# The keys' decay sums of a forgetting attention: by a thin product on TensorE for each head, or by a broadcast through memory

## The chip, the cores and the metric

One core of a Trainium2 chip. The metric is the device time of the whole program in microseconds, as the median of several executions.

## The reference

One call runs 256 tokens of width 1024, in float32, through two blocks. The first is a feed-forward layer, a mixer (chunked attention and pooling), and a second feed-forward layer. The second block is a forgetting attention ("fox") and a sparse latent attention ("dsa"), each followed by a layer norm. What is computed in the forgetting attention, with 8 heads of width 128:

```python
q, k, v, f_logit, gate = split(x @ w_in)
log_f = log_sigmoid(f_logit + b_f)                # [token, head]
cum = cumsum(log_f, axis=token)
s = (q @ k.T) * 128 ** -0.5 + cum[query, head] - cum[key, head]
s = where(key <= query, s, -inf)
o = softmax(s) @ v
y = (silu(gate) * o) @ w_out
```

So a score has three terms beside the product of query and key: a sum that belongs to the query (one number for each row of a tile of scores), a sum that belongs to the key (one number for each column, the same in all rows), and the causal mask. The change is about the second.

## The kernel before

The 256 tokens are two tiles of 128. A weight matrix is cut into units of two 128-row blocks of up to 512 columns (512 KB). SP's queue loads the units in the order of use into four buffers; ScalarE makes of each a rounded part (`whi`, line 195) and VectorE the rest (`wlo`, line 196), into eight buffers each. A product with the weights is three products on TensorE (line 162): low part of x by high part of w, high by low, high by high. Both tiles use a unit before it is given up, and the splits run up to eight units ahead of the use.

The order of the work on TensorE is written with a clock of the kernel's own: each product adds its estimated time to it, and the attention's pieces are put in a heap with a due time (the table DUE) after what they follow. After each half of a unit the pieces that are due are emitted between the products with weights. The framework's planner then fixes, before the program runs, the order of each engine's instructions and all waits and buffers; on the chip each engine works through its list in order.

The forgetting attention runs in this order: the blocks of k, q, and [f | v]; after the first block of [f | v] the logits of the gates are turned into `log_f`; `cums` (line 728) makes the running sums, and two more blocks of v pass; then the two gate blocks of the first tile, with the first tile's attention between their products, and the two of the second tile with the second's (`attend`, line 809). Scores are made in groups, of 4 heads and 128 keys for the first tile (two groups), and of 2 heads and 256 keys for the second (four groups). A group has one of the two PSUM banks that have the name `sc`; these banks serve the products with v too.

`cums` makes by small products the sums both ways: `cq`, a token to a partition, for the queries, and a copy of [8 heads, 256 keys] for the keys. Of the latter a rounded part goes to rows 0 to 7 of a tile `cum` (ScalarE), and the rest, by VectorE and GpSimd, to rows 32 to 39. `E` is a constant of 40 rows that holds -1 at a head's two rows. In `scores` (line 758) the product of E's column, broadcast to 128 columns, with `cum` puts the key's sum, negated, into all rows of the bank, and the head's own product is added to it. VectorE adds the query's sum and the mask on the way out of PSUM:

```python
self.mm(ps[:, i, :], E[:, h:h + 1].to_broadcast([40, P]), cum[:, 0:nk], True, False, 1)
if t == 0:
    self.mm(ps[:, i, :], qT[:, h, :], kT[:, h, :], False, True)
else:
    self.mm3(ps[:, i, :], qTs, kTs, False, True, (slice(None), h), (slice(None), h))
nc.vector.scalar_tensor_tensor(s[:, i, :], ps[:, i, :], cq[t][:, h:h + 1],
                               self.cmask[:, S - nk:S], op0=ALU.add, op1=ALU.add)
```

For the first tile a head's own product is one in full float32 (two records in the trace), for the second it is three of the split parts. Then come the maximum over keys (VectorE, line 419), the exponentials (ScalarE, line 421), transposes on TensorE (line 177), the product with v, and the gating.

Of the kernel before, what the change touches and what calls it, by code (L numbers as in the profile page):

```python
# [16 lines left out]
P = 128  # L17
# [18 lines left out]
# column blocks of the products with x on the left, in the order in which they are used  # L36
FFN_CH = [(512 * j, min(512, DFF - 512 * j)) for j in range((DFF + 511) // 512)]
MIX_CH = [(1536, 512), (512, 512), (0, 512), (1024, 512)]           # u k q v
FOX_CH = [(1024, 512), (1536, 512), (0, 512), (512, 512),           # k0 k1 q0 q1
          (0, 344), (344, 344), (688, 344),                          # of [f | v]  # L40
          (3080, 512), (3592, 512)]                                  # gate
DSA_CH = [(0, 372), (372, 372),                                      # of [ki | qi | wi | kr | ckv]
          (0, 512), (512, 512), (1768, 512), (2280, 512)]            # q gate


def unit_list():
    """(matrix, first k-tile, k-tiles, first column, columns) in the order of use."""
    u = []

    def block(m, c0, w, k0=0, k1=KT, n=None):  # L50
        n = n or (UK * (512 // w) if 512 % w == 0 else UK)
        for k in range(k0, k1, n):
            u.append((m, k, min(n, k1 - k), c0, w))

    def ffn(i):
        for c0, w in FFN_CH:
            block(f"gate{i}", c0, w, n=1 if i == 1 and c0 == 0 else None)
            block(f"up{i}", c0, w)
        for n in range(2):
            block(f"down{i}", 512 * n, 512, 0, FT)  # L60

    ffn(1)
    for c0, w in MIX_CH:
        block("mix", c0, w)
    for k0 in (4, 0):
        for n in range(2):
            block("mix_out", 512 * n, 512, k0, k0 + 4)
    ffn(2)
    for i, (c0, w) in enumerate(FOX_CH):
        block("fox_fv" if 4 <= i < 7 else "fox", c0, w)  # L70
    for n in range(2):
        block("fox_out", 512 * n, 512)
    for i, (c0, w) in enumerate(DSA_CH):
        block("dsa_idx" if i < 2 else "dsa", c0, w)
    for n in range(2):
        block("dsa_out", 512 * n, 512)
    return u
# [6 lines left out]
# When, in us of the tensor engine's work after what it follows, a piece of work takes its turn.  # L84
# [29 lines left out]
class Kern:  # L114
    def __init__(self, ctx, tc, A):
        self.tc, self.nc, self.A, self.ctx = tc, tc.nc, A, ctx
        pool = lambda name, **k: ctx.enter_context(tc.tile_pool(name=name, bufs=1, **k))
        self.cp = pool("const")
        self.wp = pool("w")
        self.xp = pool("x")  # L120
        self.ps = pool("ps", space=bass.MemoryType.PSUM)
        self.now = 0.0
        self.heap, self.fired, self.blocked = [], set(), {}
        self.seq = 0
        self.n_dma = self.n_split = self.used = 0
        self.raw, self.W = {}, {}
        off = 0
        self.off = []
        for (_, _, nk, _, w) in UNITS:
            self.off.append(off)  # L130
            off += P * nk * w

# [5 lines left out]
    def when(self, keys, us, fn):  # L138
        """fn, us after all of the keys are fired."""
        keys = [k for k in keys if k not in self.fired]  # L140
        if not keys:
            self.later(us, fn)
        else:
            self.blocked.setdefault(keys[0], []).append((keys[1:], us, fn))
# [23 lines left out]
    def mm3(self, out, a, b, start, stop, ai=slice(None), bi=slice(None)):  # L168
        """a.T @ b from the parts (hi, lo) of a and b, taken at ai and bi."""
        (ah, al), (bh, bl) = a, b  # L170
        self.mm(out, al[ai], bh[bi], start, False, 1)
        self.mm(out, ah[ai], bl[bi], False, False, 1)
        self.mm(out, ah[ai], bh[bi], False, stop, 1)
# [39 lines left out]
    def half(self, acc, lhs, i, first, last, kbase=0, cols=None):  # L213
        """acc += lhs.T @ unit i, for one tile of tokens; lhs: (hi, lo) of [P, k-tile, P]."""
# [18 lines left out]
    def split_psum(self, hi, lo, src, scale=None):  # L233
        """hi + lo = src (a PSUM tile), times a column for each of its blocks if scale is given."""
# [15 lines left out]
    def split_scaled(self, dst, src, f):  # L250
        """hi + lo = src f, f a column or a number."""
        hi, lo = dst
        self.nc.scalar.activation(hi, src, AF.Copy, scale=f)
        self.nc.vector.scalar_tensor_tensor(lo, src, f, hi.bitcast(F32), op0=ALU.mult, op1=ALU.subtract)
# [5 lines left out]
    def open_xT(self, t):  # L260
        """After the last product with x[t]: what follows is written to x's operand."""
# [3 lines left out]
    def put_T(self, dst, t, src, k0, n, scale=None):  # L265
        """dst k-tiles k0.. of tile t = transposed blocks of src ([P, n * P])."""
# [19 lines left out]
    def rstd(self, t, src=None, n=D, eps=EPS):  # L286
        """1 / rms of each token of x[t]."""
# [12 lines left out]
    def first_chunk(self, u0, n, pool, gain):  # L300
        """The first block: x's transposes come from memory, a pair of k-tiles at a time."""
# [26 lines left out]
    def chunk(self, u0, n, first_gain=None):  # L328
        """The product of x with one block of columns (units u0 .. u0+n), tile by tile.

        Yields t when tile t is complete. With first_gain the second half of x's transposes
        is made in between, where the vector engines have it ready."""
# [82 lines left out]
    def softmax_part(self, pool, s, nh, nk, l, col):  # L415
        """exp(s - max) for nh heads ([P, nh, nk]) in place; row sums into l[:, col..]."""
# [7 lines left out]
    def p_T(self, pool, s, nh, nk, split=False):  # L424
        """Transposes of s: [k, head, k-tile, q], or the parts of [k, k-tile, head, q]."""
# [20 lines left out]
    def mixer(self, u, gain, next_gain):  # L446
        self.stage = "mix"
        nc, tc, A = self.nc, self.tc, self.A
        with tc.tile_pool(name="mix", bufs=1, reuse_waits="tile") as pool:
# [11 lines left out]
            # of the first tile's products whole operands, of the second's the parts  # L461
# [34 lines left out]
            def scores(t, b):  # L496
                """Heads of one half of t: both halves of the array's rows at once, to two banks."""
# [104 lines left out]
    def layer_norm(self, t, o, g, b, out=None):  # L602
        """x[t] = LN(alpha x[t] + o); o: PSUM banks of 512 columns, or of 512, 256, 256."""
# [29 lines left out]
    def silu_gate(self, pool, acc, out, hr):  # L633
        """out = y (1 + tanh(z / 2)) = 2 silu(z) / (z / y); hr: half of z / y, or None for a half."""
# [5 lines left out]
    def out_proj(self, u, after, last=False):  # L640
        """o = og @ w_out, a tile at a time; after(t, (half, half))."""
# [21 lines left out]
    def fox(self, u, gain):  # L663
        self.stage = "fox"
        nc, tc, A = self.nc, self.tc, self.A
        with tc.tile_pool(name="fox", bufs=1, reuse_waits="tile") as pool:
# [6 lines left out]
            cum = pool.tile([40, S], F32R, name="cum")  # L673
            E = pool.tile([40, 8], F32R, name="E")
# [3 lines left out]
            Ef = pool.tile([40, 8], F32, name="Ef")  # L678
            nc.sync.dma_start(out=Ef, in_=A["E"])
            nc.gpsimd.tensor_copy(E, Ef)  # L680
            nc.gpsimd.memset(cum.bitcast(F32), 0.0)
# [46 lines left out]
            def cums():  # L728
# [12 lines left out]
                nc.scalar.copy(cum[0:8, :], ps[0:8, 0:S])  # L741
                nc.vector.tensor_sub(cs, ps[0:8, 0:S], cum[0:8, :].bitcast(F32))
                nc.gpsimd.tensor_copy(cum[32:40, :], cs)
# [14 lines left out]
            def scores(t, g):  # L758
# [3 lines left out]
                for i in range(nh):  # L762
                    h = g * nh + i
                    self.mm(ps[:, i, :], E[:, h:h + 1].to_broadcast([40, P]), cum[:, 0:nk], True, False, 1)
                    if t == 0:
                        self.mm(ps[:, i, :], qT[:, h, :], kT[:, h, :], False, True)
                    else:
                        self.mm3(ps[:, i, :], qTs, kTs, False, True, (slice(None), h), (slice(None), h))
                    nc.vector.scalar_tensor_tensor(s[:, i, :], ps[:, i, :], cq[t][:, h:h + 1],
                                                   self.cmask[:, S - nk:S], op0=ALU.add, op1=ALU.add)  # L770
# [38 lines left out]
    def attend(self, u, pool, gt, hr, scores, pv):  # L809
        """The two gate blocks, with the attention of both tiles between their products."""  # L810
# [25 lines left out]
    def gate_out(self, t, hb, o, l, f, gt):  # L836
        """gt = gt o f / l for four heads, and its transposes into the operand of the product out."""
# [12 lines left out]
    def dsa(self, u, x_gain=None):  # L850
        self.stage = "dsa"
        nc, tc, A = self.nc, self.tc, self.A
        with tc.tile_pool(name="dsa", bufs=1, reuse_waits="tile") as pool:
# [25 lines left out]
            def do_rope(x, n, half, t, off):  # L879
                """x: [P, n, 2 * half + rest], rotated in place."""  # L880
# [192 lines left out]
    def start(self):  # L1073
        """The first loads, those that the first product waits for ahead of the others."""
# [38 lines left out]
def shape_constants():  # L1113
    """Arrays that depend on shapes alone."""
# [15 lines left out]
    E = np.zeros((40, 8), f)  # L1130
    E[np.arange(8), np.arange(8)] = E[np.arange(32, 40), np.arange(8)] = -1.0
# [9 lines left out]
    return {"cst": cst, "avg": avg, "E": E, "rope": rope}  # L1141


def layout(inp):
    """The inputs, laid out as the kernel reads them."""
# [49 lines left out]
```

## Time and profile before

| | |
|---|---|
| time, three executions | 740.29, 741.0, 800.42 us; median 741.0 |
| span of the profiled execution | 738.3 us (its own total is not listed) |
| TensorE busy in the span | 723.9 us |
| VectorE, ScalarE, GpSimd busy | 483.4, 369.7, 21.7 us |
| granted clock of TensorE, mean | 0.996 of 2.4 GHz |

PE is TensorE, PEld its weight loads, DVE VectorE, ACT ScalarE, POOL GpSimd, and SP the engine that issues most transfers. A row of the timeline gives the start in us after the span's start, the duration, the engine, the line, the operation, output and inputs by the program's names, sizes, and in brackets idle time ahead of it and what ended it. Matmuls are pipelined and their ends are modelled, so the durations of neighbours overlap; the step from one start to the next is the better measure. A busy TensorE is one with a matmul under way, not one at its peak.

### The profile page before, as it was taken

The page shows a single profiled execution, that of the slowest core. Times are in us where ns is not written, and L with a number is a line of the kernel's source. Part 1 is how long each engine was busy: PE and PEld are TensorE (multiplying, and loading weights), DVE is VectorE, ACT ScalarE, POOL GpSimd, SP SyncE. Part 2 cuts the span into 40 slices and gives each one's busy share as a digit, 9 for nine tenths or more (in the row PEclk, how much of TensorE's full clock was granted, in tenths as well). Part 3 has the DMA queues.
Part 4 walks back from the last instruction along what each step waited for, and adds up shares of the span by engine and source line. Part 5 has one row for each costly group of instructions (what it writes and reads, how often), then busy time and mean ns, then how long its engine had stood idle before and what let it go on. Part 6 is the DMA issues. An engine that isn't in the chain of part 4 may idle for free.

```text
span 738.3 us, 9882 instructions
## 1 busy us (share of the span) xinstructions
PE 723.9 (98%) x3696; PEld 606.1 (82%) x3696; DVE 483.4 (65%) x767; ACT 369.7 (50%) x544; POOL 21.7 (3%) x29
## 2 busy tenths in 40 slices
PE   8999999999999999999999999999999999999996
PEld 6788888888888778888888888878987889778985
DVE  5775656545557867655656545565455868998865
ACT  5663544434445745453544434544563635675830
POOL 0000000000002001000000000000000000000001
PEclk9999999999999999999999999999999999999999
DMA  8886556565644335546556565655471317733401
GB/s 259 272 300 214 168 175 222 177 198 181 245 163 148 138 111 175 199 160 211 166 177 219 181 197 177 207 189 153 139 247 39 137 57 262 229 115 115 171 0 58
DMA packets 38257, 128.26 MB, mean 174 GB/s; under 512 B 4402, under 2 KB 5570, under 8 KB 38082
## 3 DMA queue, kind: packets, MB, share of 16 engines
q1 hardware_dynamic: 37890, 127.23, 52.2%
q8 instruction: 29, 0.48, 0.3%
q10 hardware_dynamic: 288, 0.39, 0.1%
q14 instruction: 18, 0.15, 0.1%
q0 software_dynamic: 32, 0.02, 0.0%
HBM read 126.57 MB, written 1.05 MB: 173 GB/s over the span
## 4 chain that ended last, share of the span: by engine, by line
PE 89%; DVE 4%; DMA 4%; ACT 2%; issue 1%; SPq 0%; POOL 0%; DVEq 0%; ACTq 0%
PE mm L162 77%; PE sc L162 6%; PE tr L177 4%; DMA raw<-in_w 2%; DVE wlo L196 1%; DMA row_final_norm<-in_final_norm 1%; PE tr L162 1%; ACT whi L195 1%; DMA x<-in_x 1%; ACT s L421 0%; ACT sq L292 0%; DVE xl L244 0%; DVE sel L958 0%; POOL rs L281 0%; DVE sel L949 0%
## 5 line engine op out<-in xcount | busy, mean ns | idle before, releaser
L196 DVE TENSOR_TENSOR wlo<-raw,whi 128x1024 fp32r<-128x1024 f32 (+3 forms) x236 | 276.4, 1177 | 133.0 <-ACT whi L195 126.7
L195 ACT CAST whi<-raw 128x1024 fp32r<-128x1024 f32 (+3 forms) x236 | 238.4, 1014 | 194.9 <-PE mm L162 170.3
L162 PE MATMUL mm<-whi,xl 128*128 128x512 f32 (+3 forms) x760 | 290.1, 383 | 2.4 <-ACT whi L195 1.2
L162 PE MATMUL mm<-wlo,xh 128*128 128x512 f32 (+3 forms) x760 | 284.2, 374 | 0.4 <-DVE wlo L196 0.4
L162 PE MATMUL mm<-whi,xh 128*128 128x512 f32 (+3 forms) x760 | 283.4, 373 | 0.0
L162 PEld LDWEIGHTS mm<-whi,xl 128*128 128x128 f32 x760 | 143.4, 189 | 25.8 <-ACT whi L195 1.6
L162 PEld LDWEIGHTS mm<-whi,xh 128*128 128x128 f32 x760 | 143.3, 189 | 24.4
L162 PEld LDWEIGHTS mm<-wlo,xh 128*128 128x128 f32 x760 | 143.6, 189 | 23.1 <-DVE wlo L196 1.7
L162 PE MATMUL mm<-whi,hl 128*128 128x512 f32 x176 | 69.0, 392 | 0.0
L162 PE MATMUL mm<-whi,hh 128*128 128x512 f32 x176 | 68.5, 389 | 0.0
L162 PE MATMUL mm<-wlo,hh 128*128 128x512 f32 x176 | 68.5, 389 | 0.0
L162 PEld LDWEIGHTS mm<-whi,hh 128*128 128x128 f32 x176 | 33.0, 188 | 6.9
L162 PEld LDWEIGHTS mm<-wlo,hh 128*128 128x128 f32 x176 | 33.1, 188 | 6.6
L162 PEld LDWEIGHTS mm<-whi,hl 128*128 128x128 f32 x176 | 33.1, 188 | 6.6
L392 DVE SCALAR_TENSOR_TENSOR h<-a,qr,mm 128x512 f32<-128x512 f32 (+1 forms) x24 | 16.8, 698 | 20.4 <-PE mm L162 20.4
L421 ACT ACTIVATE s<-s,nmax 128x128 f32<-128x128 f32 (+1 forms) x48 | 21.3, 445 | 12.3 <-DVE nmax L419 12.3
L237 ACT CAST hh<-tr 128x512 fp32r<-128x512 f32 (+1 forms) x24 | 13.1, 547 | 25.6 <-PE tr L177 25.5
L238 DVE TENSOR_TENSOR hl<-tr,hh 128x512 fp32r<-128x512 f32 (+1 forms) x24 | 15.4, 641 | 16.0 <-ACT hh L237 16.0
L383 ACT ACTIVATE th<-mm,hr 128x512 f32<-128x512 f32 (+1 forms) x24 | 15.7, 653 | 16.2 <-PE mm L162 11.3
L385 DVE SCALAR_TENSOR_TENSOR a<-th,mm 128x512 f32<-128x512 f32 (+1 forms) x24 | 15.3, 638 | 7.8 <-ACT th L383 7.8
L237 ACT CAST xh<-tr 128x512 fp32r<-128x512 f32 x12 | 6.9, 588 | 19.1 <-PE tr L177 19.0
L281 POOL TENSOR_TENSOR rs<-ms,mhalf 128x1 f32<-128x1 f32 x10 | 6.4, 643 | 327.6 <-DVE ms L294 327.6
(222 smaller groups left out, 589.5 us busy)
## 6 DMA issues: line engine op xcount, KB each, us to landing
raw<-in_w SPq DMA_DIRECT2D x208, 512.0 KB, 4.3
raw<-in_w SPq DMA_DIRECT2D x12, 344.0 KB, 3.2
raw<-in_w SPq DMA_DIRECT2D x8, 372.0 KB, 3.9
raw<-in_w SPq DMA_DIRECT2D x8, 256.0 KB, 4.7
x<-in_x SPq DMA_DIRECT2D x2, 512.0 KB, 4.7
B<-in_bias SPq DMA_DIRECT2D x1, 1024.0 KB, 5.5
row_ln_g<-in_ln_g SPq DMA_DIRECT2D x2, 512.0 KB, 6.8
row_ln_b<-in_ln_b SPq DMA_DIRECT2D x2, 512.0 KB, 6.3
```

Of the source, the lines that this page charges most:

```text
L162: self.nc.tensor.matmul(out, a, b, start=start, stop=stop)
L177: self.nc.tensor.transpose(out, a, self.ident[:p, :p])
L195: nc.scalar.copy(hi[:, :m], raw[:, :m])
L196: nc.vector.tensor_sub(lo[:, :m], raw[:, :m], hi[:, :m].bitcast(F32))
L237: nc.scalar.copy(hi, src)
L238: nc.vector.tensor_sub(lo, src, hi.bitcast(F32))
L281: self.nc.gpsimd.tensor_tensor(out, a, self.mhalf[:, 0:1].to_broadcast(list(a.shape)), op=ALU.pow)
L383: nc.scalar.activation(th[:, :w], acc[:, :w], AF.Tanh, scale=hr[t])
L385: nc.vector.scalar_tensor_tensor(a[t][:, :w], th[:, :w], 1.0, acc[:, :w], op0=ALU.add, op1=ALU.mult)
L392: nc.vector.scalar_tensor_tensor(h[:, :w], a[t][:, :w], qr[t], acc[:, :w], op0=ALU.mult, op1=ALU.mult)
L421: nc.scalar.activation(s[:, h, :], s[:, h, :], AF.Exp, bias=m[:, h:h + 1], accum_out=l[:, col + h:col + h + 1])
```

## The change

The thin products, E and `cum` go. ScalarE copies the sums with a factor of -1 to `cs`. GpSimd's queue writes these 8 KB to memory and reads them back twice, the first and the last 128 keys, each time broadcast to all 128 partitions, into a tile `ck` of [128, 8 heads, 256 keys]. GpSimd adds the causal mask of the diagonal block: to the first half for the first tile, into a tile `ck0` of its own, and to the second half in place. VectorE's score instruction then adds a head's row of `ck0` or `ck` where it added the mask. The head's own product is the first into its part of the bank.

```diff
     def __init__(self, ctx, tc, A):
+        self.dp = pool("d", space=bass.MemoryType.DRAM)
...
     def fox(self, u, gain):
-            cum = pool.tile([40, S], F32R, name="cum")
-            E = pool.tile([40, 8], F32R, name="E")
+            ck = pool.tile([P, 8, S], F32, name="ck")
+            ck0 = pool.tile([P, 8, P], F32, name="ck0")
             bf = self.row(pool, "b_f", 8)
             fg = self.row(pool, "final_norm")
             lg, lb = self.row(pool, "ln_g0"), self.row(pool, "ln_b0")
-            Ef = pool.tile([40, 8], F32, name="Ef")
-            nc.sync.dma_start(out=Ef, in_=A["E"])
-            nc.gpsimd.tensor_copy(E, Ef)
-            nc.gpsimd.memset(cum.bitcast(F32), 0.0)
...
             def cums():
                 cs = pool.tile([8, S], F32, name="cs")
-                nc.scalar.copy(cum[0:8, :], ps[0:8, 0:S])
-                nc.vector.tensor_sub(cs, ps[0:8, 0:S], cum[0:8, :].bitcast(F32))
-                nc.gpsimd.tensor_copy(cum[32:40, :], cs)
+                nc.scalar.activation(cs, ps[0:8, 0:S], AF.Copy, scale=-1.0)
+                d = self.dp.tile([8, S], F32, name="ck")
+                nc.gpsimd.dma_start(out=d, in_=cs)
+                diag = self.cmask[:, None, P:S].to_broadcast([P, 8, P])
+                for k in range(2):
+                    c = slice(k * P, (k + 1) * P)
+                    nc.gpsimd.dma_start(out=ck[:, :, c], in_=d[None, :, c].to_broadcast([P, 8, P]))
+                nc.gpsimd.tensor_tensor(ck0, ck[:, :, 0:P], diag, op=ALU.add)
+                nc.gpsimd.tensor_tensor(ck[:, :, P:S], ck[:, :, P:S], diag, op=ALU.add)
                 self.fire(("fox", "cum"))
...
             def scores(t, g):
-                    self.mm(ps[:, i, :], E[:, h:h + 1].to_broadcast([40, P]), cum[:, 0:nk], True, False, 1)
                     if t == 0:
-                        self.mm(ps[:, i, :], qT[:, h, :], kT[:, h, :], False, True)
+                        self.mm(ps[:, i, :], qT[:, h, :], kT[:, h, :], True, True)
                     else:
-                        self.mm3(ps[:, i, :], qTs, kTs, False, True, (slice(None), h), (slice(None), h))
+                        self.mm3(ps[:, i, :], qTs, kTs, True, True, (slice(None), h), (slice(None), h))
                     nc.vector.scalar_tensor_tensor(s[:, i, :], ps[:, i, :], cq[t][:, h:h + 1],
-                                                   self.cmask[:, S - nk:S], op0=ALU.add, op1=ALU.add)
+                                                   (ck if t else ck0)[:, h, :], op0=ALU.add, op1=ALU.add)
```

The constant E goes from the inputs too, and comments are taken out throughout. The DUE table is not changed; without the thin products the kernel's own clock runs 1.3 us less over the scores.

## Rows read from the trace of the kernel before

**Rows 1.** The page's first part: engine, busy us, share of the span, instructions.
```profile
PE 723.9 (98%) x3696; PEld 606.1 (82%) x3696; DVE 483.4 (65%) x767; ACT 369.7 (50%) x544; POOL 21.7 (3%) x29
```

**Rows 2.** Busy by stretch: PE, PEld, DVE, ACT, POOL; clock; DMA share, GB/s.
```profile
525.60:548.80 23.20, 23.20 (x150) 22.55 (x149) 13.06 (x22) 15.44 (x22) 1.26 (x1) 1.00 0.63 211
548.80:566.50 17.70, 17.70 (x83) 13.60 (x82) 8.91 (x19) 7.45 (x22) 0.00 (x0) 1.00 0.34 116
```

**Rows 3.** Tile E, and a wait of PEld (total us, times, longest).
```profile
L162 PE MATMUL sc<-cum,E x16: 322/352/382, 552.1 to 578.8; 40*128 40x128 f32 x8, 40*128 40x256 f32 x8
...
PEld sc L162 <- issue: 3.9, 15, 0.4
```

**Rows 4.** Timeline of PE, the first tile's first scores: start us, us, instruction.
```profile
551.57 0.39 PE L162 MATMUL mm<-wlo,xh 128*128 128x512 f32 x1
551.80 0.39 PE L162 MATMUL mm<-whi,xh 128*128 128x512 f32 x1
552.12 0.32 PE L162 MATMUL sc<-cum,E 40*128 40x128 f32 x1
552.37 0.49 PE L162 MATMUL sc<-kT,qT 128*128 128x128 f32 x2
552.79 0.32 PE L162 MATMUL sc<-cum,E 40*128 40x128 f32 x1
553.04 0.49 PE L162 MATMUL sc<-kT,qT 128*128 128x128 f32 x2
553.28 0.48 PE L162 MATMUL mm<-whi,xl 128*128 128x512 f32 x1
553.69 0.32 PE L162 MATMUL sc<-cum,E 40*128 40x128 f32 x1
```

**Rows 5.** Timeline of PE, two places in the second tile's scores.
```profile
567.55 0.38 PE L162 MATMUL sc<-cum,E 40*128 40x256 f32 x1
...
568.32 0.39 PE L162 MATMUL mm<-whi,xl 128*128 128x512 f32 x1
...
573.34 0.40 PE L162 MATMUL mm<-whi,xh 128*128 128x512 f32 x1
573.67 0.38 PE L162 MATMUL sc<-cum,E 40*128 40x256 f32 x1
```

**Rows 6.** Timeline of PE, scores of the sparse attention.
```profile
684.16 0.28 PE L162 MATMUL sc<-ckvTsh,qlTsl 128*128 128x256 f32 x1
...
684.52 0.28 PE L162 MATMUL sc<-ks,qs 96*128 96x256 f32 x1
684.64 0.28 PE L162 MATMUL sc<-ckvTsh,qlTsl 128*128 128x256 f32 x1
```

**Rows 7.** Timeline of DVE, the first score instruction (idle time in brackets).
```profile
552.90 0.35 DVE L769 SCALAR_TENSOR_TENSOR s<-sc,cq,cst 128x128 f32<-128x128 f32 x1 [1.60 <-PE sc L162]
```

**Rows 8.** Timelines of ACT and POOL, the keys' sums.
```profile
539.66 0.36 ACT L741 CAST cum<-tr 8x256 fp32r<-8x256 f32 x1
...
541.46 1.26 POOL L743 CAST cum<-cs 8x256 fp32r<-8x256 f32 x1 [57.88 <-DVE cs L742]
```

**Rows 9.** DMA issues: count, KB each, median us to landing.
```profile
row_final_norm<-in_final_norm SPq DMA_DIRECT2D x1, 512.0 KB, 6.4
...
out<-x SPq DMA_DIRECT2D x2, 256.0 KB, 2.0
xin<-in_xT SPq DMA_DIRECT2D x2, 128.0 KB, 3.1
...
gain<-in_gain POOLq DMA_DIRECT2D x1, 19.0 KB, 3.4
```

**Rows 10.** Timeline of POOL, its one load and a copy.
```profile
1.23 0.71 POOL L1076 DMA_DIRECT2D gain<-in_gain  x1 [0.79 <-POOLq L1187]
...
643.22 0.29 POOL L899 COPY kid<-y 128x128 f32<-128x128 f32 x1 [14.15 <-DVE y L891]
```

**Rows 11.** Timeline of DVE, the first use of the final norm's row.
```profile
480.60 1.28 DVE L707 SCALAR_TENSOR_TENSOR x<-x,rs,row_final_norm 128x1024 f32<-128x1024 f32 x1 [1.48 <-DMA row_final_norm<-in_final_norm]
```

More of the change, by code (lines that the diff above doesn't have):

```diff
@@ L1129, in shape_constants @@
         avg[:, 1024 + 16 * g:1024 + 16 * (g + 1)] = m[:P, P:P + 16]
-    E = np.zeros((40, 8), f)
-    E[np.arange(8), np.arange(8)] = E[np.arange(32, 40), np.arange(8)] = -1.0
     rope = np.zeros((P, 2, 96), f)
@@ L1140, in shape_constants @@
         o += rot
-    return {"cst": cst, "avg": avg, "E": E, "rope": rope}
+    return {"cst": cst, "avg": avg, "rope": rope}
 def layout(inp):
```

## The prediction

> **What bounds the kernel now.** I read the busy totals first, then the chain of waits, then the busy time by stage, then TensorE's own rows in the attention of the forgetting layer. TensorE is busy for 723.9 of 738.3 us [rows 1], and the chain of work that ended last is nearly all TensorE. The totals alone could hide a stage with another limit, so I looked at the two stages that the change touches: the last value block before the scores, and the gate block with the first tile's scores. TensorE is busy for the whole of both, 23.2 of 23.2 us and 17.7 of 17.7 us, at a granted clock of 1.00, which is the 2.4 GHz level, while VectorE and ScalarE have gaps [rows 2]. So whatever TensorE time the change really removes there comes off the end, unless a new wait is put into TensorE's in-order queue. Busy does not mean well used: the question is what a 40-row product costs as a step from start to start, since the recorded durations overlap their neighbours.
>
> **What goes: the 40-row products.** There are 16 of them, eight with 128 columns for the first tile and eight with 256 for the second; their weight loads stood idle beforehand 15 times, 3.9 us in all, with nothing released [rows 3]. That says these loads are not hidden behind the product before, as the others are.
>
> First tile, from start to start [rows 4]. From such a product to the head's own product it is 552.37 - 552.12 = 0.25 us. From a head's product (two records, one step) to the next 40-row product it is 552.79 - 552.37 = 0.42, where the same head's product followed by a gate product takes 553.28 - 553.04 = 0.24; so 0.18 is the way into the 40-row product. From a gate product into it is 552.12 - 551.80 = 0.32 against 551.80 - 551.57 = 0.23 between gate products: 0.09. The pattern of two heads and one gate product stands four times: 4 x (2 x 0.25 + 0.18 + 0.09) = 3.1 us.
>
> Second tile [rows 5]: from the 40-row product to the first product after the head is 568.32 - 567.55 = 0.77. The same three products of 256 columns in the sparse attention, with nothing ahead of them, take 684.52 - 684.16 = 0.36 [rows 6]. That leaves 0.41, and 0.33 - 0.23 = 0.10 for the way in (573.34 to 573.67): 0.51, eight times, 4.1 us. The sum is 7.2 us. Its lower bound is what a thin product costs where it does not break the flow: the 96-row product of the sparse attention takes 684.64 - 684.52 = 0.12 us [rows 6], 16 x 0.12 = 1.9 us. I take 7.2, since its rows are those of the very instructions that go.
>
> The Trainium skill, "TensorE: Matmul & The Clock Gate", section "Back-to-back issue gap", gives a matmul N / 2.4 + 2.5 ns at the full clock, so these 16 would be worth 8 x 56 + 8 x 109 ns = 1.3 us, an estimate from that page, and by it the time would be 739.7. The rows above disagree by a factor of five.
>
> Also gone: a small load on SP's queue, its cast and a memset on GpSimd, and on VectorE one subtraction of 8x256. The copy of the sums on ScalarE stays, with a factor [rows 8]. I cost these at nothing: all lie beside a busy TensorE. With that cover gone the subtraction would give back about what the copy of the same 8x256 takes, 0.36 us [rows 8], and the others no more.
>
> **What comes: the path of the keys' sums.** Before, the sums were ready at 542.7 (GpSimd's cast, 541.46 + 1.26), nine microseconds ahead of the first use at 552.1 [rows 4, 8]. Now they go ScalarE, memory, two broadcasts, and two additions on GpSimd, all in GpSimd's order: write, first half, second half, add, add.
> - ScalarE's copy ends at 539.66 + 0.36 = 540.0 [rows 8].
> - The 8 KB write: 2.0 us like the stores of the output, up to 3.4 like the one load from GpSimd's queue [rows 9]. I take 3.4, the same queue: 543.4.
> - One half is 512 KB in 1024 pieces of 512 bytes. No row shows that. The final norm's row, 512 KB to all partitions in pieces of 4 KB, landed in 6.4 us; the first 128 KB loads, 256 pieces of 512 bytes, in 3.1 [rows 9]. With 2.0 fixed and 1.1 for each 256 pieces it is 2.0 + 4 x 1.1 = 6.4 as well. Bounds: 3.1, and 4 x 3.1 = 12.4. I take 6.4, on which both rows agree: 549.8.
> - Issuing: GpSimd was busy 0.71 us for a load of 128 rows [rows 10]. If that grows with the pieces it is 8 x 0.71 = 5.7 us for each half, and the first addition stands behind both issues. I take 0.71, the only row, and keep 5.7 for the range.
> - An addition of 128x1024 on GpSimd: a 128x128 copy took 0.29, so 2.3 [rows 10]; the cast took 1.26 for 256 columns [rows 8], so 5.0 at most. I take 2.3, since the cast ran beside VectorE's splits.
>
> The first tile's keys are then ready at 549.8 + 2.3 = 552.1; bounds 542.0 + 3.1 + 0.3 = 545.4 (the addition no longer than that copy) and, with both issues at 5.7, the landing at 12.4 and the addition at 5.0, about 566. VectorE's first use was at 552.90 [rows 7], now some 0.25 earlier, 552.65. So it comes out even. Who waits if it is late: VectorE stops at the first score instruction, and behind it stand the other scores, the maxima, ScalarE's exponentials, and TensorE itself, because each head's product writes into a bank of two that VectorE must have read first. Gate products can fill the time only as far as the planner put them there, and it fixes the order ahead of time, with its own idea of when a transfer lands. It has misjudged one: VectorE stood 1.48 us for the final norm's row with other work behind it [rows 11]. I charge one such error, 1.5 us; bounds 0 and 566 - 552.65 = 13.4. Below nothing I exclude, since a wait adds no speed.
>
> The second half, issued 0.7 us after the first, lands perhaps at 556, and its addition ends near 559; the second tile's scores began at 567.55 [rows 5], and begin at about 565 if the first tile gives back its 3.1 us. That cover is 6 us, and the additions stand on an idle GpSimd. The extra megabyte falls where the DMA share is 0.63 and then 0.34 [rows 2], and eight weight units are split ahead, so I charge nothing for late weights; without that cover one late unit costs what a landing takes, 3 to 6 us [rows 9]. The larger tiles move others in memory; the rows loaded from memory move behind the freed area, which can only take waits away.
>
> The sum: 738.3 - 7.2 + 1.5 = 732.6 us of span. The profiled execution's own total is not listed beside its span; the median, 741.0, lies 2.7 above it, and I keep that: **735.3 us**.
>
> **The rivals.**
> 1. The keys come late, and the kernel is slower. Place: VectorE's first score instruction. It decides from the point where the wait is longer than 7.2 us, that is, keys later than 552.65 + 7.2 = 559.9. For it: 1024 small pieces for each half, on GpSimd's own queue, and the additions behind two issues. Against it: the planner can move gate products ahead of the scores, and a tile's two gate blocks hold 48 of them (2 blocks, 8 k-tiles, 3 products), 11 us at 0.23. At the upper bound the time is 741.0 - 7.2 + 13.4 = 747.2.
> 2. No wait at all, the whole 7.2 us: 733.8. For it: the central sum leaves 0.5 us, and the planner knows of the transfers. The Trainium skill, "DMA: Bandwidth & Descriptors", section "Anatomy of one DMA — SWDGE (gpsimd) path", fits 2.0 us plus bytes over 436e3 per us, 3.2 us for a half, whatever the pieces: keys early, and this rival's time. No run here shows that figure.
> 3. The price is not in the 40-row product but in changing over between the kinds of product around it, which stays. Then only the products' own steps go, 1.9 us: 739.1. For it: the head's products of the first tile are of another kind than the gate's. Against it: the sparse attention mixes the same kinds with steps of 0.12 [rows 6], and the skill's figure above, which would end close by, is not borne out.
> 4. The change doesn't do what it says: a product remains or another is added. The diff leaves none, so it gets no more than the remainder; its time would be that of before, 741.0.
>
> **How the numbers follow.** Forecast, a short wait of 0 to 4 us: 0.50. Rival 1: 0.18. Rival 2: 0.15. Rival 3: 0.13. Anything else: 0.04. Rival 2's lower end, with a little luck of the order, is 732.5. Rival 3 lies inside. From rival 1 I take in waits up to 8 us, 742, about a third of its chance; with that about 0.16 stays outside. The range is 732.5 to 742. Two per cent, about what a measurement of this kernel can tell from no change, is 14.8 us: 726.2 and 755.8. No case reaches either; two at once, or what I have not seen, get 0.03 on each side, and 0.94 is for no change by that measure.
>
> **What would show it.** Right: TensorE's steps in the score stretch fall to 0.24 and 0.36 per head, TensorE's instruction count falls by 16, and the first score instruction on VectorE waits a microsecond or two for GpSimd's addition. Wrong at the path: GpSimd's two issues last for microseconds each, the first addition starts after 555, and TensorE has an idle stretch ahead of the second score product. Wrong at the gain: steps between the heads' products stay at 0.4 and more. A TensorE that is idle for over 7 us between 545 and 570 would make the kernel slower; a gain over 9 us would need a wait elsewhere to vanish, of which I see none.

## The result and the profile after

The changed kernel takes 736.7 us, median of 20 executions, against 740.4 for the kernel before on the same chip: a ratio of 0.995, 95% interval [0.9937, 0.9964], so 3.7 us less with 2.7 to 4.7 as its bounds, and no change by the two per cent. The forecast was 735.3 in a range of 732.5 to 742.

The profiled execution is the slowest of the 20, 739.97 us with a span of 738.2, so its span against that of before hides the gain. What the change did to a stage is read between two fixed pieces of TensorE's work instead: the first transposes of k in the forgetting layer, and the second tile's transposes at the start of the sparse layer.

The kernel before, timeline of PE (start us, us, instruction, idle time in brackets), with one gate product that is used further down:
```profile
484.91 0.44 PE L177 MATMUL tr<-cst,y 128*128 128x128 f32 x2 [1.17 <-ACT y L687]
...
559.72 0.39 PE L162 MATMUL mm<-wlo,xh 128*128 128x512 f32 x1
...
621.96 1.29 PE L177 MATMUL tr<-cst,x 128*128 128x128 f32 x8
```
The changed kernel, timeline of PE: the same two pieces, the first tile's first scores between them, a gate product behind them, one head of the second tile, and two transposes of the sparse layer:
```profile
485.20 0.44 PE L178 MATMUL tr<-cst,y 128*128 128x128 f32 x2 [1.56 <-ACT y L685]
...
552.37 0.60 PE L163 MATMUL sc<-kT,qT 128*128 128x128 f32 x4
552.73 0.48 PE L163 MATMUL mm<-whi,xl 128*128 128x512 f32 x1
553.04 0.40 PE L163 MATMUL mm<-wlo,xh 128*128 128x512 f32 x1
555.71 0.75 PE L163 MATMUL sc<-kT,qT 128*128 128x128 f32 x4 [2.27 <-DVE s L772]
...
559.94 0.39 PE L163 MATMUL mm<-wlo,xh 128*128 128x512 f32 x1
...
569.92 0.28 PE L163 MATMUL sc<-kTsh,qTsl 128*128 128x256 f32 x1
...
570.28 0.40 PE L163 MATMUL mm<-whi,xh 128*128 128x512 f32 x1
...
619.66 1.29 PE L178 MATMUL tr<-cst,x 128*128 128x128 f32 x8 [0.44 <-DVE x L624]
...
627.64 0.63 PE L178 MATMUL tr<-cst,y 128*128 128x128 f32 x4 [1.24 <-DVE y L893]
...
642.98 0.63 PE L178 MATMUL tr<-cst,y 128*128 128x128 f32 x4 [2.12 <-DVE y L894]
```
From piece to piece it was 621.96 - 484.91 = 137.05 us before and 619.66 - 485.20 = 134.46 after: 2.6 less. The thin products are gone (PE has 3680 instructions where it had 3696): two heads of the first tile (four records) and the way to the next gate product take 552.73 - 552.37 = 0.36 us where they took 553.28 - 552.12 = 1.16 [rows 4], and a head of the second tile 570.28 - 569.92 = 0.36 where it took 0.77 [rows 5]. And there is one new wait, 2.27 us ahead of the third head's product. The chain of waits of the changed kernel, followed back from there (start us, us, what):
```profile
540.67 2.66 DMA ck<-cs
...
543.87 8.21 DMA ck<-ck
...
552.16 3.12 POOL ck L746
...
555.30 0.36 DVE s L772
...
555.71 0.75 PE sc L163 x4
```
The wait is where the prediction put it: VectorE's first score instruction, held by GpSimd's addition. It was put at 1.5. The keys came at 552.16 + 3.12 = 555.28 instead of 552.1. After the wait something comes that the prediction did not have. The windows of the changed kernel (columns as in [rows 2]):
```profile
548.80:552.00 3.20, 3.20 (x16) 2.63 (x15) 1.56 (x3) 1.44 (x3) 0.00 (x0) 1.00 1.01 315
552.00:556.00 4.00, 1.73 (x11) 1.22 (x10) 1.67 (x3) 1.11 (x1) 3.84 (x2) 1.00 1.02 398
556.00:560.00 4.00, 4.00 (x18) 3.58 (x18) 1.78 (x6) 0.69 (x1) 1.58 (x1) 0.57 0.21 84
```
In the four microseconds after TensorE stood idle it was granted 0.57 of its clock, by single microseconds 0.68, 0.50, 0.50 and 0.61, that is, the 1.2 GHz level for most of it, where the kernel before was at 1.00 throughout [rows 2]. At half speed the work of these 4 us is 4 x (1 - 0.57) = 1.7 us late, an estimate that the first experiment below bears out. So the profiled sum is -7.2 + 2.27 + 1.7 + 0.44 (the idle time ahead of the transposes at 619.66) = -2.8, beside the measured -2.6. What was left at 619.66 this one execution lost again in the sparse layer: TensorE waited 1.24 and 2.12 us for VectorE, where before it waited only at the second place, 1.34. Half of the executions are over 3.2 us faster than this one, so that is not the median's story.

### The profile page after: what moved, and what is told of

It reads as the page before. It is cut to its first block, busy times and chain, and to the rows that moved or that the text cites. A ratio compares the mean times of both kernels' runs of the same rounds, so it can differ in the third digit from the quotient of the medians.

```text
span 738.2 us, 9854 instructions
## 1 busy us (share of the span) xinstructions
PE 719.9 (98%) x3680; PEld 605.7 (82%) x3680; DVE 482.5 (65%) x766; ACT 369.9 (50%) x544; POOL 27.9 (4%) x31
## 4 chain that ended last, share of the span: by engine, by line
PE 80%; issue 9%; DMA 4%; DVE 3%; ACT 1%; POOL 1%; SPq 0%; DVEq 0%; POOLq 0%; ACTq 0%
PE mm L163 70%; PE sc L163 5%; PE tr L178 4%; DMA raw<-in_w 2%; DMA rope<-in_rope 1%; DMA ck<-ck 1%; DVE wlo L197 1%; ACT whi L196 1%; PE tr L163 1%; ACT s L422 0%; POOL ck L746 0%; DMA ck<-cs 0%; POOL rs L282 0%; DVE sel L961 0%; DVE sel L952 0%
```

## The experiments

Each kernel was timed against the kernel before on the same chip.

**The thin products alone taken out.** The changed kernel without the key path; the score instruction adds the mask alone, so the keys' sums are left out of the result.

```diff
-                d = self.dp.tile([8, S], F32, name="ck")
-                nc.gpsimd.dma_start(out=d, in_=cs)
...
-                nc.gpsimd.tensor_tensor(ck0, ck[:, :, 0:P], diag, op=ALU.add)
-                nc.gpsimd.tensor_tensor(ck[:, :, P:S], ck[:, :, P:S], diag, op=ALU.add)
...
-                        (ck if t else ck0)[:, h, :], op0=ALU.add, op1=ALU.add)
+                        self.cmask[:, S - nk:S], op0=ALU.add, op1=ALU.add)
```

> The changed kernel without the write, the two broadcasts and the two additions; the score instruction adds the plain mask, so the keys' sums are left out of the scores. Theory A (the thin products are worth 7.2 us on TensorE, 2.3 of them lost to the late keys, about 1.6 to the half clock behind that wait, and some given back at the start of the sparse attention, which waits for its tables and weights from memory): no idle stretch and no half clock in the scores, the second tile's transposes ahead of the sparse attention begin 6 to 7.5 us earlier than before (621.96), and the time lies 4 to 7 us under the kernel before, depending on how much is given back. Theory B (the thin products were worth only the 3.8 us that the change gained; the wait costs nothing): 3 to 4.5 us under the kernel before, as the changed kernel.

733.8 us against 740.9, ratio 0.9901 [0.9873, 0.9929]. In its timeline of PE:
```profile
482.48 0.44 PE L178 MATMUL tr<-cst,y 128*128 128x128 f32 x2 [0.23 <-ACT y L683]
...
549.61 0.60 PE L163 MATMUL sc<-kT,qT 128*128 128x128 f32 x4
...
553.13 0.39 PE L163 MATMUL mm<-wlo,xh 128*128 128x512 f32 x1
...
612.27 1.29 PE L178 MATMUL tr<-cst,x 128*128 128x128 f32 x8
```
612.27 - 482.48 = 129.79, 7.26 us less than before. The price of the 16 products is what the steps gave, 7.2, and it reaches the end whole. This kernel runs the same products in the same order as the changed one, so it also prices the wait and the clock: from the first score product to the same gate product it is 553.13 - 549.61 = 3.52 us here and 559.94 - 552.37 = 7.57 in the changed kernel, 4.05 more, of which 2.27 is the wait and about 1.7 the clock.

**The key path alone added.** The kernel before, with the write, the broadcasts and the additions of the change beside its thin products; nobody reads the path's result.

```diff
                 nc.gpsimd.tensor_copy(cum[32:40, :], cs)
+                d = self.dp.tile([8, S], F32, name="ck")
+                nc.gpsimd.dma_start(out=d, in_=cum[0:8, :].bitcast(F32))
...
```

> The kernel before, with the thin products kept, and in addition the write, both broadcasts and both additions, whose result nobody reads (the rounded part of the sums is what is sent). Theory A: nobody waits for them, so no change, within 1 us. Rival C (the extra megabyte and the additions on GpSimd slow the weights or VectorE): 2 to 4 us slower than before, with TensorE waiting for a split or ScalarE for a weight load between 545 and 570.

747.5 us, ratio 1.0084 [1.0053, 1.0116]: 6.6 us slower, more than either theory had, though no score waits for a key. Its timelines of ACT, DVE and PE:
```profile
552.58 1.05 ACT L196 CAST whi<-raw 128x1024 fp32r<-128x1024 f32 x1 [4.14 <-DMA raw<-in_w]
...
553.66 1.82 DVE L197 TENSOR_TENSOR wlo<-raw,whi 128x1024 fp32r<-128x1024 f32 x1 [4.03 <-ACT whi L196]
555.41 0.59 DVE L780 SCALAR_TENSOR_TENSOR s<-sc,cq,cst 128x128 f32<-128x128 f32 x2
...
551.88 0.32 PE L163 MATMUL sc<-cum,E 40*128 40x128 f32 x1
...
555.80 0.47 PE L163 MATMUL sc<-cum,E 40*128 40x128 f32 x1 [2.27 <-DVE s L780]
...
565.95 0.40 PE L163 MATMUL mm<-wlo,xh 128*128 128x512 f32 x1
```
and its windows:
```profile
552.00:556.00 4.00, 1.73 (x8) 1.15 (x8) 2.34 (x3) 2.33 (x2) 3.57 (x2) 0.91 0.82 329
556.00:560.00 4.00, 4.00 (x11) 2.65 (x11) 0.99 (x4) 0.00 (x0) 1.69 (x1) 0.50 0.41 150
560.00:566.50 6.50, 6.50 (x20) 4.93 (x20) 2.90 (x8) 3.00 (x15) 0.00 (x0) 0.57 0.00 0
```
With the broadcasts under way a weight block landed 4.1 us after ScalarE was ready for it. Its split stands in VectorE's queue ahead of the first scores, so the scores, and TensorE behind them, waited 2.27 us for a block that no product needed yet. Then TensorE was granted 0.91, 0.50 and 0.57 of its clock, the middle one the 1.2 GHz level throughout. What this cost is read from the products, which are the same in the same order as in the kernel before: from the first thin product to the same gate product it is 565.95 - 551.88 = 14.07 us here and 559.72 - 552.12 = 7.60 before [rows 4], 6.5 more. That is the 6.6 by which the time rose, so 2.3 is the wait and about 4.2 the clock.

**The scores later, with and without the change.** Three kernels with 4 us added to the due times of the first tile's scores in the table DUE, so that more gate products stand ahead of them: the changed kernel, the kernel with both, and the kernel before as a control.

```diff
-    "fox_s": (2.04, 2.43, 0.8, 2.8, 6.38, 6.5),
+    "fox_s": (6.04, 6.43, 0.8, 2.8, 6.38, 6.5),
```

> The changed kernel with the first tile's scores due 4 us later in the table, so that 18 gate products move ahead of them and the keys have 4 us more. Theory A: the wait of 2.3 us and the half clock disappear; the second tile's transposes ahead of the sparse attention begin 3 to 4 us earlier than in the changed kernel (619.66 there), and the time is 0 to 4 us below the changed kernel, that is 4 to 7 us under the kernel before. Theory B: the wait costs nothing, so the time stays 3 to 4.5 us under the kernel before.

> The kernel before with the whole key path added beside its products, the path's result unread (as in the run that did so at +6.6 us), but with the planner told that the first tile's scores may start 4 us later. If the loss of that run came from where its wait fell (a late weight block's split held up in VectorE's queue ahead of the scores, and TensorE's clock at half afterwards): most of it goes, 741 to 743. If the loss is the transfers' load itself (a megabyte of broadcasts taking the DMA engines from the weights): it stays, 746 to 748.

> The kernel before, with the planner told that the first tile's scores may start 4 us later, nothing else. Control for the changed kernel with later scores, which came to 732.9. If that gain is the key path's wait removed: no change here, 740.9 within 1.5. Rival (a later start of the scores is worth something by itself, whatever makes the key sums): 737 to 738, the same 3.8 us as it gave on the changed kernel.

The changed kernel: 732.9 us, ratio 0.9899 [0.9871, 0.9927], whose interval does not overlap that of the 0.995 [0.9937, 0.9964] of the change as it was, and which is within 0.0002 of the kernel with no key path at all. The kernel with both: 741.1, ratio 1.0009 [0.9994, 1.0024]; its 6.6 us are gone. The control: 740.3, ratio 1.0003 [0.9987, 1.002]; a later start is worth nothing by itself. So both the wait and the clock that follows it hang on where the scores stand, and there the megabyte of broadcasts costs nothing clear of the noise (0.0024 of 740.4, 1.8 us, at the interval's end). In the profiled execution of the kernel with both and later scores, ScalarE stood 1.74 us for the late block and not 4.14, so what a block as late as that would do there is not shown. The changed kernel with later scores, timelines of POOL, DVE and PE:
```profile
552.29 2.40 POOL L746 TENSOR_TENSOR ck<-ck,cst 128x1024 f32<-128x1024 f32 x1 [6.92 <-DMA ck<-ck]
554.65 3.35 POOL L747 TENSOR_TENSOR ck<-ck,cst 128x1024 f32<-128x1024 f32 x1
...
552.45 3.31 DVE L197 TENSOR_TENSOR wlo<-raw,whi 128x1024 fp32r<-128x1024 f32 x1 [2.53 <-ACT whi L196]
...
556.65 0.61 DVE L772 SCALAR_TENSOR_TENSOR s<-sc,cq,ck 128x128 f32<-128x128 f32 x2 [0.29 <-issue]
...
614.75 1.03 PE L178 MATMUL tr<-cst,x 128*128 128x128 f32 x8
```
and its windows:
```profile
552.00:556.00 4.00, 4.00 (x20) 3.30 (x19) 3.55 (x2) 2.39 (x3) 3.71 (x2) 1.00 0.89 353
556.00:560.00 4.00, 4.00 (x27) 3.30 (x26) 2.72 (x10) 0.00 (x0) 2.01 (x1) 1.00 0.39 147
```
The keys come at 554.7, the scores start at 556.65 and wait for no key, TensorE is busy throughout and its clock stays at 1.00. From its first transposes of k, at 484.96, to the second tile's at 614.75 it is 129.79, the value without a key path.

**The sparse layer's tables loaded later.** One theory had the lost part given back at the start of the sparse layer, where the loads of two tables would meet an earlier start. They are moved behind the first two weight blocks, in the changed kernel and in the one with later scores.

```diff
-            nc.sync.dma_start(out=wuk, in_=A["w_uk"])
-            nc.sync.dma_start(out=wuv, in_=A["w_uv"])
...
             u += 8
+            nc.sync.dma_start(out=wuk, in_=A["w_uk"])
+            nc.sync.dma_start(out=wuv, in_=A["w_uv"])
```

> The changed kernel with the two 512 KB tables of the sparse attention (w_uk, w_uv) issued after its first two weight blocks are done, instead of ahead of them and of the rope table. Theory A: the rope table lands some 4 us earlier, the wait of 1.2 us for it ends, the weights behind it come earlier too, and the time is 1 to 3 us below the changed kernel, 5 to 7 us under the kernel before. If nothing is given back there: as the changed kernel, 3 to 4.5 us under the kernel before.

> The changed kernel with the first tile's scores 4 us later in the planner (that alone: 732.9), and with the two tables of the sparse attention loaded after its first two weight blocks (that alone: no gain over the changed kernel). If the tables' loads never stood on the path: 732.9 within 1. If they do once the scores no longer wait, because the sparse layer then starts 7 us earlier: 730 to 731.5.

738.8 us, ratio 0.9964 [0.9945, 0.9982], and 733.6, ratio 0.9906 [0.9886, 0.9926]: no better than without the move in either. The tables are not where the gain went.

**What makes a thin product dear.** Four kernels that change only the thin products of the kernel before. Three fill them up with rows of zeros, to 128, 72 and 64 (the diff shows 128); one keeps the 40 rows and writes the selecting column out 128 times, in place of reading one column with a stride of zero.

```diff
-            cum = pool.tile([40, S], F32R, name="cum")
-            E = pool.tile([40, 8], F32R, name="E")
+            cum = pool.tile([P, S], F32R, name="cum")
+            E = pool.tile([P, 8], F32R, name="E")
...
-                    self.mm(ps[:, i, :], E[:, h:h + 1].to_broadcast([40, P]), cum[:, 0:nk], True, False, 1)
+                    self.mm(ps[:, i, :], E[:, h:h + 1].to_broadcast([P, P]), cum[:, 0:nk], True, False, 1)
```

> The kernel before, with the 16 thin products over 128 rows instead of 40: the sums and the selecting array are padded with zero rows, so the result and the count of products are unchanged. Theory P (the price of a thin product is its 40 rows: a weight load of another number of rows than its neighbours' can't run beside the product before it): the loads overlap as the others do, a product costs what the 96-row one of the sparse attention does, 16 x 0.12 = 1.9 us of the 7.26, so the time falls by 5.3, to about 735.5 from 740.9. Rival Q (the price is in the weights being one column repeated 128 times, read with a stride of zero): nothing changes, 740.9 within 1.5. Rival R (the price is in changing over between kinds of product): nothing changes here either, and nothing in the run with the 40 rows written out.

> The kernel before, with the selecting weights written out in memory as 128 columns for each head, in place of one column repeated; still 40 rows, same products. Theory P (40 rows): nothing, 740.9 within 1.5. Rival Q (the repeated column makes the load slow): the time falls by about 5.3, to 735.5. Rival R (changing over between kinds of product): nothing, 740.9.

> The kernel before, with its 16 thin products over 64 rows (zero rows added to the 40). With 128 rows the time fell by 4.7 us, to 735.7; with 40 it is 740.4. Theory P1 (the price is paid by a product that fits into half the array's rows, since the array is then set up for another division of its rows): 64 rows cost what 40 do, 740.4 within 1.5. Theory P2 (the price is paid in proportion to the rows missing from 128): 64 of 128 gives back 24 of the 88 missing rows, 1.3 us, 739.1. Theory P3 (any count that is a whole multiple of 32 rows runs on, 40 does not): 735.7.

> The kernel before, with its 16 thin products over 72 rows (zero rows added to the 40). Theory P1 (only a product that fits into half the array's rows pays): the whole gain of the 128 rows, 4.7 us, 735.7. Theory P2 (in proportion to the missing rows): 32 of 88 given back, 1.7 us, 738.7. Theory P3 (whole multiples of 32 only): nothing, 740.4.

| rows of a thin product | time, us | ratio to before |
|---|---|---|
| 40, column written out | 741.3 | 1.002 [1.0003, 1.0036] |
| 64 | 740.9 | 0.9998 [0.9984, 1.0013] |
| 72 | 734.9 | 0.9917 [0.99, 0.9934] |
| 128 | 735.7 | 0.9931 [0.9911, 0.9951] |
| no product (first experiment) | 733.8 | 0.9901 [0.9873, 0.9929] |

It is a step, not a slope: 64 rows cost what 40 do, 72 what 128 do. The timeline of PE with 72 rows, the last two heads of the first tile between the two fixed pieces:
```profile
482.54 0.44 PE L177 MATMUL tr<-cst,y 128*128 128x128 f32 x2 [0.48 <-ACT y L688]
...
552.73 0.33 PE L162 MATMUL sc<-cum,E 72*128 72x128 f32 x1
552.89 0.43 PE L162 MATMUL sc<-kT,qT 128*128 128x128 f32 x2
553.08 0.31 PE L162 MATMUL sc<-cum,E 72*128 72x128 f32 x1
553.23 0.44 PE L162 MATMUL sc<-kT,qT 128*128 128x128 f32 x2
553.42 0.48 PE L162 MATMUL mm<-whi,xl 128*128 128x512 f32 x1
...
614.26 1.25 PE L177 MATMUL tr<-cst,x 128*128 128x128 f32 x8
```
its weight loads as a group (busy, mean ns, idle time before and what ended it):
```profile
L162 PEld LDWEIGHTS sc<-cum,E 72*128 72x128 f32 x16 | 3.0, 188 | 0.9 <-DVE s L770 0.6
```
and the group of weight loads in the kernel before, whose numbers the kernel with the 40 rows written out repeats:
```profile
L162 PEld LDWEIGHTS sc<-cum,E 40*128 40x128 f32 x16 | 2.9, 182 | 3.5 <-issue 1.3 <-DVE s L769 0.7 <-DVE g L844 0.5
```
Two heads take 553.42 - 552.73 = 0.69 us with 72 rows and 1.16 with 40 [rows 4], though there are more rows to load; and the idle time ahead of the thin products' own loads falls from 3.5 us to 0.9, with the 1.3 in which nothing was released gone. Between the fixed pieces the kernel with 72 rows takes 614.26 - 482.54 = 131.72 us, 5.33 less than the kernel before. Here a product of 40 or 64 rows, which fits into half of the array's 128, broke the flow on the way in and on the way out; one of 72 or 128 did not, and zeros did for rows. The Trainium skill, "TensorEngine Tiling (Array Packing)", section "Key Properties", says that a change of the tiling mode drains TensorE, and the page's list of configurations, in its section "Available Configurations", has one of twice 64 rows. The 64 and the 72 rows agree with that; that it is a drain no row here shows.

## Why the prediction was right, and where its sizes were off

**The gain.** 7.2 us from steps between starts; 7.26 between the fixed pieces without a key path, and 0.0099 of 740.9, 7.3, in the medians. Reading steps and not durations was what made it so. The lower bound, 16 x 0.12 = 1.9 us for products that do not break the flow, turns out to have a meaning of its own: it is what stays when the products are filled up, 7.3 - 6.1 = 1.2 with 72 rows and 7.3 - 5.1 = 2.2 with 128 by the ratios, and 131.72 - 129.79 = 1.93 with 72 rows between the fixed pieces. So of 7.2 us about 5.3 were the price of the half array. One row was misread, though nothing in the sum hangs on it: the 3.9 us and 15 times of [rows 3] count every load for a bank `sc`, the heads' own and those of other stages too; the thin products' loads have 1.3 of it. Rival 3, that only 1.9 would go, fell with the first experiment. So did the 1.3 us worked out from the Trainium skill, "TensorE: Matmul & The Clock Gate", section "Back-to-back issue gap", whose formula is for a single product taken by itself: the 1.2 to 2.2 us of the filled-up products lie about there, the 7.2 do not.

**The path.** Every term was within its bounds, and the sum was 3.2 us short: ready at 555.3, not 552.1. The three terms that were added up account for 1.9 of it; the other 1.3 passed between the steps, which the sum put at nothing: 0.65 ahead of the write (it began at 540.67, not 540.02), and 0.5 between its landing and the first issue at 543.87.

| term | predicted | measured |
|---|---|---|
| write of 8 KB | 3.4 | 2.66 |
| first half, from issue to landing | 6.4 | 8.21 |
| addition | 2.3 | 3.12 |
| issue of a half | 0.71 | 0.9 |

The issues of the changed kernel's DMA view (KB each, median us to landing):
```profile
ck<-ck POOLq DMA_DIRECT2D x2, 512.0 KB, 8.5
ck<-cs POOLq DMA_DIRECT2D x1, 8.0 KB, 2.7
```
The landing was taken from transfers of the start and of the final norm; here the DMA engines were at a share of 1.01 and 1.02, full with weights and broadcasts at once. Whether the pieces or that competition made 8.2 of 6.4, no run separates; the median of the two halves, 8.5 here, was 8.0 to 10.0 us in the five experiments that have them. The addition's 3.12 reads as 2.2 of its own and 0.9 of waiting; the additions that started ahead of a split took 2.35 and 2.40. VectorE's split ran from 551.84 to 553.07:
```profile
551.84 1.23 DVE L197 TENSOR_TENSOR wlo<-raw,whi 128x1024 fp32r<-128x1024 f32 x1 [1.64 <-ACT whi L196]
555.30 0.61 DVE L772 SCALAR_TENSOR_TENSOR s<-sc,cq,ck 128x128 f32<-128x128 f32 x2 [2.24 <-POOL ck L746]
```
and 553.07 + 2.2 is where the addition ends. In the kernel with later scores the two take turns in plain sight: the split, 1.2 us elsewhere, lasts 3.31 because it ends 1.1 after the first addition (554.69), and the second addition lasts 3.35 because it ends 2.2 after the split (555.76). The Trainium skill, "SBUF — State Buffer", section "Who interferes with whom", says that a VectorE instruction with two inputs from SBUF contends with a GpSimd one that reads there, that the lock on the shared ports is exclusive, and that the order of issue decides who waits; these rows agree.

**The wait.** Charged at 1.5 us, measured at 2.27. The cause given was an order fixed ahead of time that has the scores before the keys. That was right: with 4 us more in the table it loses nothing. That the planner misjudged a landing is not shown; what stood too early was the kernel's own due time, which the change left as it was. The size was taken from another wait, and by the sum's own figures (keys at 552.1, first use at 552.65) there would have been none. So 1.5 for 2.27 is in part luck. Of the signs of being wrong at the path, the idle stretch ahead of a score product came, at the third head; the first addition did start ahead of 555, at 552.16. Rival 1, that the keys come late by more than the gain, did not come about, but it came more than half way: 2.3 us of wait and 1.7 of clock make 4.0 of the 7.2. Rival 2, no wait at all, fell with the 2.27: a half landed after 8.21 us and not 3.2.

**What the sum lacked.** The granted clock after the wait. I counted an idle TensorE as the idle time and no more; it cost 1.7 us on top in the changed kernel and 4.2 in the one with both. The two errors, path and clock, add 0.8 + 1.7 = 2.5 us of cost to the profiled sum. As a gain the forecast was 741.0 - 735.3 = 5.7 us, and 3.7 was measured, 2.0 short. As a time it is off by only 1.4, 736.7 for 735.3, because the kernel before came to 740.4 and not 741.0; that part is luck.

**What was costed at nothing.** The subtraction, cast and small load: the kernel with no key path gains the 7.3 of the products and no more, so nothing. The extra megabyte: wrongly argued. "Eight weight units are split ahead" did not keep a split from being late; the late split stood in front of the scores, and where these came at that moment it cost 6.6 us, clock and all. In the changed kernel the keys were later than that split, so it did not show. The second half: its addition ended at 555.24 + 2.35 = 557.6, ahead of the 559 predicted, and nobody waited.

**Best version.** The changed kernel with later scores, 732.9, ratio 0.9899 [0.9871, 0.9927]. With the products filled up to 72 rows, no key path and no new transfer, the kernel before comes to 0.9917 [0.99, 0.9934], which these runs do not tell apart from that, and which is ahead of the change as it was, 0.995 [0.9937, 0.9964].

## What to carry to other kernels

Price a product by the step from start to start among its neighbours, not by the idle time that a profile puts down to its loads: 16 products of 40 rows between full ones cost here 0.45 us each, 64 rows cost no less, and zero rows up to 72 or 128 took 5 to 6 of the 7.3 us away. Try such padding before a new path: here it gave more than the change as it was. When a transfer takes over work from TensorE, look at what is queued ahead of and behind its consumer, the late weight splits too, and leave the consumer room for a late landing; here 4 us of due time were worth another 3.8 us, as much as the change itself. And count a stall of TensorE with the clock that it loses afterwards, here 1.7 and 4.2 us behind waits of 2.27.

## What was not expected of the hardware

- A wait of 2.27 us was followed by 0.57 of the clock over 4 us in one kernel, and by 0.50 over 4 us and 0.57 over 6.5 more in another, with the same length of wait ahead. Why the second lasted longer is open; its TensorE had the thin products between its others, which may or may not be the reason.
- The price of a thin product is a step between 64 and 72 rows; neither the stride of zero nor the number of missing rows beyond that step showed in the time.
- A split of 1.2 us on VectorE became 3.3 beside an addition on GpSimd, and GpSimd's addition of 2.2 to 2.4 became 3.1 and 3.35 beside a split.
